# Two layers of a retention, HGRN2 and differential attention block: the 16-bit planes of the values are parted and joined on ScalarE instead of GpSimd

## Chip, cores and metric

The kernel runs on one core of a Trainium2 chip. The metric is the device time of one execution in microseconds (us). Of several executions the median is taken. A profiled execution gives the trace; its engines are called TensorE (PE), VectorE (DVE), ScalarE (ACT), GpSimd (POOL) and SyncE (SP, here only a queue that issues transfers).

## What is computed

A sequence of 16 learned tokens and 256 inputs (272 tokens, width 1024) goes through two layers. Each layer is a mixer and a convolutional feed-forward network, both with a residual and an RMS norm:

```python
proj = hn @ w_in                      # 12 parts: rq rk rv rg | hq hf hi hg | dq dk dv | mg
o_ret = retention(rq, rk, rv, rg)     # 4 heads, scores x fixed decay, values rv (256 wide)
o_hg  = hgrn2(hq, hf, hi, hg)         # 8 heads, decay from the data, values hi (128 wide)
o_da  = diff_attention(dq, dk, dv)    # 8 heads, two softmaxes, values dv (128 wide)
y = sum(sigmoid(mg)[n] * (o[n] @ w_branch[n]) for n in (ret, hg, da))
h = h + y @ w_out
...
u = rms_norm(h) @ w_ffn_in            # 2 x 2816 wide
c = causal convolution of width 3 over the tokens
h = h + (silu(gate) * val) @ w_ffn_out
```

All inputs and results are float32. The output is the normed last 256 tokens.

## The kernel before

**Layout.** Activations lie transposed in SBUF: the partitions hold 128 features, the free dimension the 272 tokens. A projection takes 128 x 128 weight tiles as the stationary operand and 272 tokens as the moving one. In the second layer most projections leave out the first 14 tokens (258 columns).

**Weights.** To keep float32 accuracy, every weight tile and every activation is split into a rounded high part and a remainder, and each product is made of three matmuls (lines 915 to 917: high with high, high with low, low with high). The weights come as one stream of chunks of 8 tiles (class `_Weights`, method `next`, line 626). For each chunk the SP queue loads `wraw` (3 buffers), ScalarE copies it to `whi` (4 buffers) and VectorE subtracts to get `wlo` (4 buffers). So for each chunk there is a chain: load, ScalarE, VectorE, TensorE. A load must wait until VectorE is done with the chunk three before, a split until TensorE is done with the chunk four before.

**Order of the projections.** `ORDER` (line 63) lists pairs of output tiles in the order in which TensorE makes them. Marks among them start (`+`) and end (`!`) the work of the heads that is spread between the projections: `hga` and `hgb` are the two groups of four HGRN2 heads, `hgoa` and `hgob` their outputs, `ret` the retention heads, `daa` and `dab` the attention heads.

**The values.** The heads need the values with tokens on the partitions, so the projections `rv`, `hi` and `dv`, 4 pairs of tiles each, must be transposed: 12 pairs in a layer, 24 in all. `values` (line 1389) evacuates a pair from PSUM to `vsrc` on ScalarE, and `to_tokens` (line 951) transposes its first 256 tokens. Each float32 is treated as two 16-bit halves. The lower and upper halves are parted into two planes (`apart`), each plane is transposed by a DMA issued from the SP queue (`turned`), and the two planes are joined again into float32 words in `vt` (or `rvt`). Parting and joining are plain copies with a step of two 16-bit words on one side, 512 elements in each partition; each is one instruction for each plane. The last 16 tokens of a pair go another way: GpSimd gathers them in `tails`, and TensorE transposes those.

**The level chain of HGRN2.** `hg_heads` (line 1064) computes the data-dependent decay by levels of 1, 2, 4, ... 64 tokens. At each level TensorE multiplies blocks of keys and queries (`lev`, line 1107), VectorE puts the masked result into `near`, and VectorE then multiplies the next level's decays into `hq` and `hf` in place. Before that, on the four lowest levels, ScalarE copies the last tokens of `hf` and `hq` to `kt` and `qt`, and once a larger part of `hq` to `extra`. At the end ScalarE copies the blocks to `at`. Retention and HGRN2 outputs take their norm over partitions by an all-reduce on GpSimd (`hr`), with ScalarE before and after it.

**The planner.** The kernel does not issue instructions as the program text runs. Class `_Plan` (line 357) collects them with their dependences, a due time (`key`) and a cost, plays the engines forward as a list scheduler (`order`, line 454), and issues everything in the order found. Each engine then works through its own list in that order, and waits where an operand isn't ready. The costs are fixed in the code:

```python
act = _Engine(plan, nc.scalar, "act", 0.094, 0.833e-3)
...
pool = _Engine(plan, nc.gpsimd, "pool", 0.04, 0.85e-3)
sync = _Engine(plan, nc.sync, "sp", 0.06, 4 / 360e3)
```

To these come, for GpSimd, 1.6e-3 us for each element in a partition (line 592), and for a transfer 2.0 us from the end of its issue to landing (line 546). For a copy of 512 elements the planner thus reckons 0.52 us on ScalarE and 1.29 us on GpSimd, for the transpose of a plane 0.79 us on the SP queue and 2.0 us more.

Of the kernel before, what the change touches and what calls it, by code (L numbers as in the profile page):

```python
# [16 lines left out]
AF = mybir.ActivationFunctionType  # L17
# [4 lines left out]
P = 128  # L22
# [644 lines left out]
def _trace(ctx, tc, plan, a, depth, probe):  # L667
    nc = tc.nc
    act = _Engine(plan, nc.scalar, "act", 0.094, 0.833e-3)
    dve = _Engine(plan, nc.vector, "dve", 0.068, 1.042e-3)  # L670
    pe = _Engine(plan, nc.tensor, "pe", 0.0, 4 / 2400)
    pool = _Engine(plan, nc.gpsimd, "pool", 0.04, 0.85e-3)
# [14 lines left out]
    def new(pool_, shape, dt, tag, bufs, name):  # L687
        serial[0] += 1
        return plan.tile(pool_, shape, dt, tag, bufs, f"{name}_{serial[0]}")
# [16 lines left out]
    def temp2(tag, bufs=2):  # L706
        return temp(2 * T, tag, bufs).rearrange("p (a t) -> p a t", a=2)
# [243 lines left out]
    def to_tokens(src, vt, e):  # L951

        def planes(name):
            return new(tp, [P, 4 * T], U16, "vsrc", 4, name)[:, : 8 * P].rearrange("p (i x) -> p i x", i=2)

        apart, turned = planes("apart"), planes("turned")
        halves = lambda t, i: t.bitcast(U16).rearrange("p a (x two) -> p a x two", two=2)[:, :, :, i]
        for i in range(2):
            pool.tensor_copy(apart[:, i].rearrange("p (c f x) -> p c f x", c=2, f=2),
                             halves(src[:, :, : 2 * P], i).rearrange("p f (c x) -> p c f x", c=2))  # L960
        for i in range(2):
            sync.dma_start(turned[:, i].rearrange("p (b x) -> p b x", x=P), apart[:, i], transpose=True)
        for i in range(2):
            pool.tensor_copy(halves(vt[:, :, e : e + 2 * P], i), turned[:, i].rearrange("p (c x) -> p c x", c=2))

    def tail_tokens(tails):

# [21 lines left out]
    for li in range(depth):  # L989
# [399 lines left out]
        def values(ps, vt, e):  # L1389

            src = temp2("vsrc", 4)
            evacuate(src, ps)
            plan.key += 2.0
            to_tokens(src, vt, e)
            return src
# [57 lines left out]
        for name, j in ORDER:  # L1453
# [31 lines left out]
            if name in BASE:  # L1485
# [23 lines left out]
                elif name == "rv":  # L1509
# [3 lines left out]
                    src = values(ps, st["rvt"][j // 2], (j % 2) * 2 * P)  # L1513
# [4 lines left out]
                elif name in ("hi", "dv"):  # L1518
# [7 lines left out]
                    src = values(ps, st[f"{n}t{b}"], (j % 2) * 2 * P)  # L1526
# [39 lines left out]
            elif name == "fi":  # L1566
# [10 lines left out]
                c = temp2("two_b")  # L1577
# [8 lines left out]
                c = c[:, :, first:]  # L1586
# [43 lines left out]
```

## Time and profile before

| | |
|---|---|
| median of 3 runs | 1304.77 us (1304.16 to 1307.01) |
| the profiled execution | 1305.7 us |
| its span, first to last instruction | 1303.9 us |
| mean granted TensorE clock | 0.998 of full speed |
| busy: PE, DVE, ACT, POOL | 99%, 76%, 60%, 21% of the span |
| chain that ended last: PE, DVE, ACT | 88%, 9%, 1% of the span |
| HBM read | 216.16 MB, 167 GB/s over the span |

How to read the rows below: a row of a group names the line, the engine, the operation, output and inputs with their shapes (partitions x elements), the count, then busy time, the mean of one in ns, and the idle time of the engine just ahead of them with what ended it. Most operations pass through one helper, so line 607 stands for many; the tile names tell them apart. A row of the waits names who waited for whom, the total in us, how often, and the longest. A row of the timeline has start and duration in us, and in brackets the idle time ahead of it. Matmuls are pipelined and their records overlap, so a busy TensorE is not one at its peak, and spans on GpSimd are rough.

### The profile page before, as it was taken

To read this page: it belongs to the slowest core of one execution; us is meant where nothing else is said; L and a number is where in the kernel's file an instruction comes from. 1 tells how busy PE (TensorE), PEld (TensorE's weight loads), DVE (VectorE), ACT (ScalarE), POOL (GpSimd) and SP (SyncE) were. 2 spreads that over 40 slices of the span, in tenths; PEclk is the share of its full clock that TensorE was granted. 3 is DMA by queue.
4 is the path that set the end of the run, shared out by engine and by line. 5 is a ranking of instruction groups with operands and counts; after the bars stand their busy time and mean duration, and the time that the engine had idled before them with its cause. 6 is when DMAs were issued, how large, how long until landed. Compare 5 with 4: busy or idle time off the path is not lost.

```text
span 1303.9 us, 28637 instructions
## 1 busy us (share of the span) xinstructions
PE 1285.8 (99%) x11678; PEld 1256.7 (96%) x11678; DVE 986.7 (76%) x1589; ACT 786.7 (60%) x1282; POOL 270.3 (21%) x300
## 2 busy tenths in 40 slices
PE   9999999999999999999999999999999999999998
PEld 9999989999999999999999999899999999999986
DVE  7685897798686789886575768877986867898843
ACT  6746444746576567666456474447466765776643
POOL 5021262423422020000030212634223220200000
PEclk9999999999999999999999999999999999999999
DMA  7664665643744545555555646655446446466653
GB/s 272 200 179 147 173 178 155 164 160 125 199 138 157 182 156 178 183 173 183 175 178 185 186 149 185 179 155 168 159 138 199 145 162 198 144 207 196 201 190 112
DMA packets 86868, 225.36 MB, mean 173 GB/s; under 512 B 32976, under 2 KB 33104, under 8 KB 86736
## 3 DMA queue, kind: packets, MB, share of 16 engines
q1 hardware_dynamic: 86448, 223.00, 55.3%
q8 instruction: 92, 1.51, 0.5%
q10 hardware_dynamic: 288, 0.52, 0.1%
q14 instruction: 40, 0.33, 0.1%
HBM read 216.16 MB, written 1.05 MB: 167 GB/s over the span
## 4 chain that ended last, share of the span: by engine, by line
PE 88%; DVE 9%; issue 1%; ACT 1%; DMA 0%; SPq 0%; DVEq 0%; ACTq 0%
PE main L915 26%; PE main L917 26%; PE main L916 25%; DVE wlo L607 2%; PE fo L1430 2%; PE fo L1431 2%; PE fo L1429 2%; DVE two_b L607 1%; DVE two_a L607 1%; PE lev L1107 1%; PE ds L1291 1%; PE ho L607 1%; PE ro L607 1%; PE do L607 1%; DVE two_c L607 1%
## 5 line engine op out<-in xcount | busy, mean ns | idle before, releaser
L915 PE MATMUL main<-xh,whi 128*128 128x272 f32 (+1 forms) x2368 | 682.6, 288 | 0.8 <-ACT whi L607 0.8
L917 PE MATMUL main<-xh,wlo 128*128 128x272 f32 (+1 forms) x2368 | 673.9, 285 | 1.3 <-DVE wlo L607 0.7
L916 PE MATMUL main<-xl,whi 128*128 128x272 f32 (+1 forms) x2368 | 673.3, 284 | 1.5 <-DVE xl L607 1.5
L607 DVE TENSOR_TENSOR wlo<-wraw,whi 128x1024 fp32r<-128x1024 f32 (+1 forms) x411 | 512.0, 1250 | 187.8 <-ACT whi L607 186.6
L607 ACT ACTIVATE whi<-wraw 128x1024 fp32r<-128x1024 f32 (+1 forms) x411 | 427.5, 1042 | 250.9 <-PE main L916 166.3
L917 PEld LDWEIGHTS main<-xh,wlo 128*128 128x128 f32 x2368 | 446.5, 189 | 3.1 <-DVE wlo L607 2.3
L916 PEld LDWEIGHTS main<-xl,whi 128*128 128x128 f32 x2368 | 446.6, 189 | 2.2 <-DVE xl L607 1.9
L915 PEld LDWEIGHTS main<-xh,whi 128*128 128x128 f32 x2368 | 446.7, 189 | 2.0 <-ACT whi L607 1.0
L607 POOL TENSOR_TENSOR y<-h,rstd 128x272 f32<-128x272 f32 x32 | 34.6, 1112 | 318.1 <-ACT rstd L607 318.1
L607 POOL PARTITION_ALL_REDUCE hr<-hsq x36 | 65.8, 1837 | 88.9 <-ACT hsq L607 85.9
L607 DVE SCALAR_TENSOR_TENSOR two_b<-main,small,two_b 128x256 f32<-128x256 f32 (+2 forms) x144 | 65.3, 487 | 24.4 <-ACT two_b L607 22.7
L607 POOL COPY apart<-vsrc 128x512 uint16<-128x512 uint16 x48 | 40.7, 867 | 145.2 <-ACT vsrc L607 145.0
L607 ACT ACTIVATE two_b<-main,small 128x272 f32<-128x272 f32 (+1 forms) x72 | 37.3, 566 | 23.8 <-PE main L917 22.7
L915 PE MATMUL main<-ghi,whi 128*128 128x272 f32 x176 | 51.0, 290 | 0.0
L916 PE MATMUL main<-glo,whi 128*128 128x272 f32 x176 | 50.6, 287 | 0.0
L917 PE MATMUL main<-ghi,wlo 128*128 128x272 f32 x176 | 50.3, 286 | 0.0
L607 POOL COPY vt<-turned 128x512 uint16<-128x512 uint16 x32 | 37.0, 1160 | 29.2 <-DMA turned<-apart 29.0
L915 PE MATMUL main<-b0hi,whi 128*128 128x272 f32 (+1 forms) x128 | 37.9, 296 | 0.0
L915 PE MATMUL main<-b1hi,whi 128*128 128x272 f32 (+1 forms) x128 | 37.8, 296 | 0.0
L915 PE MATMUL main<-yhi,whi 128*128 128x272 f32 (+1 forms) x128 | 36.4, 284 | 0.0
L917 PE MATMUL main<-b0hi,wlo 128*128 128x272 f32 (+1 forms) x128 | 36.4, 284 | 0.0
L917 PE MATMUL main<-yhi,wlo 128*128 128x272 f32 (+1 forms) x128 | 36.3, 284 | 0.0
(235 smaller groups left out, 1970.1 us busy)
## 6 DMA issues: line engine op xcount, KB each, us to landing
wraw<-in_w SPq DMA_DIRECT2D x402, 512.0 KB, 3.4
h<-in_h SPq DMA_DIRECT2D x4, 272.0 KB, 5.1
dec<-in_dec SPq DMA_DIRECT2D x2, 544.0 KB, 4.9
wraw<-in_w SPq DMA_DIRECT2D x4, 256.0 KB, 4.2
const<-in_const SPq DMA_DIRECT2D x1, 937.0 KB, 5.6
turned<-apart SPq DMA_TRANSPOSE x48, 4.0
gain<-in_gl SPq DMA_DIRECT2D x1, 512.0 KB, 5.1
out<-y ACTq DMA_DIRECT2D x2, 256.0 KB, 2.8
```

What stands on the lines that cost most here:

```text
L607: self.plan.add(self.name, lambda: f(*args, **kw), cost, outs, ins, args[2] if method == "activation" else None)
L915: nc.tensor.matmul(o, wh, hi, start=first, stop=False)
L916: nc.tensor.matmul(o, wh, lo, start=False, stop=False)
L917: nc.tensor.matmul(o, wl, hi, start=False, stop=last)
L1107: nc.tensor.matmul(o, keys, x, start=True, stop=True)
L1291: nc.tensor.matmul(ss[m][:, at : at + nk], q[half, hd, q0 : q0 + P], k[half, hd, :nk], start=True, stop=True)
L1429: nc.tensor.matmul(o, gh, wh, start=False, stop=False)
L1430: nc.tensor.matmul(o, gl, wh, start=False, stop=False)
L1431: nc.tensor.matmul(o, gh, wl, start=False, stop=end)
```

## The change

In `to_tokens`, the two partings and the two joinings of each pair become ScalarE activations with the function Copy; nothing else of the text changes. Shapes, tiles, buffers and the transposes' queue stay as they are. The planner, which knows each engine's costs, lays out a new order for all engines.

```diff
         for i in range(2):
-            pool.tensor_copy(apart[:, i].rearrange("p (c f x) -> p c f x", c=2, f=2),
-                             halves(src[:, :, : 2 * P], i).rearrange("p f (c x) -> p c f x", c=2))
+            act.activation(apart[:, i].rearrange("p (c f x) -> p c f x", c=2, f=2),
+                           halves(src[:, :, : 2 * P], i).rearrange("p f (c x) -> p c f x", c=2), AF.Copy)
         for i in range(2):
             sync.dma_start(turned[:, i].rearrange("p (b x) -> p b x", x=P), apart[:, i], transpose=True)
         for i in range(2):
-            pool.tensor_copy(halves(vt[:, :, e : e + 2 * P], i), turned[:, i].rearrange("p (c x) -> p c x", c=2))
+            act.activation(halves(vt[:, :, e : e + 2 * P], i), turned[:, i].rearrange("p (c x) -> p c x", c=2), AF.Copy)
```

## The prediction

> **What bounds the kernel now.** I read the page first, then the busy time by stage, then what TensorE itself waited for, then the operations that the change touches and those around them. The first two lines of the page:
>
> ```profile
> span 1303.9 us, 28637 instructions
> ...
> PE 1285.8 (99%) x11678; PEld 1256.7 (96%) x11678; DVE 986.7 (76%) x1589; ACT 786.7 (60%) x1282; POOL 270.3 (21%) x300
> ```
>
> TensorE is busy but for 18.1 us. A change to another engine can therefore save little; it can only cost what it puts ahead of TensorE. The operations to be moved lie in a few stages, and the busy time by stage shows them:
>
> ```profile
> core 0: us, PE busy (x) PEld busy (x) DVE busy (x) ACT busy (x) POOL busy (x), PEclk, DMA share, GB/s
> ...
> 150.00:180.00 30.00, 28.56 (x344) 27.85 (x342) 26.73 (x38) 15.39 (x25) 19.28 (x21) 1.00 0.74 198
> 180.00:210.00 30.00, 29.27 (x491) 28.49 (x492) 27.38 (x46) 13.93 (x24) 11.91 (x14) 1.00 0.73 176
> ...
> 240.00:266.00 26.00, 25.19 (x202) 24.85 (x201) 20.61 (x27) 18.89 (x28) 16.12 (x17) 1.00 0.59 151
> ...
> 830.00:860.00 30.00, 28.28 (x476) 27.27 (x474) 25.79 (x43) 12.67 (x23) 16.30 (x18) 0.94 0.76 185
> ...
> 895.00:917.00 22.00, 22.00 (x180) 21.83 (x178) 16.63 (x19) 15.57 (x26) 16.09 (x17) 1.00 0.59 165
> ```
>
> From 150 to 210 us and again around 830 to 860 VectorE is about 90% full while ScalarE is half idle; from 240 to 266 and 895 to 917 ScalarE is itself about 72% full (18.89 of 26, 15.57 of 22), and these are the stages with the least room for more. TensorE's own waits between 60 and 1000 us, where all values are handled:
>
> ```profile
> PE lev L1107 <- DVE hf L607: 3.2, 2, 1.7
> PE ho L607 <- DVE ho L607: 1.4, 2, 0.8
> ...
> PE lev L1107 <- DVE tot L607: 0.4, 1, 0.4
> PE lev L1107 <- DVE hq L607: 0.4, 1, 0.4
> ```
>
> They are few, and most are the level products (lev), which wait for VectorE.
>
> **What is moved, and its price.** 48 partings and 48 joinings (two 16-bit planes, 12 pairs of value tiles, 2 layers) leave GpSimd for ScalarE's queue.
>
> ```profile
> L607 POOL COPY apart<-vsrc 128x512 uint16<-128x512 uint16 x48 | 40.7, 867 | 145.2 <-ACT vsrc L607 145.0
> ```
>
> ```profile
> L607 POOL COPY vt<-turned 128x512 uint16<-128x512 uint16 x32 | 37.0, 1160 | 29.2 <-DMA turned<-apart 29.0
> L607 POOL COPY rvt<-turned 128x512 uint16<-128x512 uint16 x16 | 15.7, 1011 | 27.7 <-DMA turned<-apart 27.7
> ```
>
> ```profile
> L607 ACT ACTIVATE whi<-wraw 128x1024 fp32r<-128x1024 f32 (+1 forms) x411 | 427.5, 1042 | 250.9 <-PE main L916 166.3
> ```
>
> ```profile
> L607 ACT ACTIVATE extra<-hq 128x512 f32<-128x512 f32 x8 | 5.4, 675 | 3.5 <-DVE hq L607 3.5
> ```
>
> GpSimd is freed of 40.7 + 37.0 + 15.7 = 93.4 us. The trace has no 16-bit copy on ScalarE; the nearest row is a strided copy between SBUF tiles of the same 512 elements, 0.675 us. At that price ScalarE gains 96 x 0.675 = 65 us and goes from 786.7 to about 852. From below, half of what a split of 1024 elements takes (1.042 us) would be 0.52 us and 50 us in all; from above, if ScalarE needed what GpSimd needed for a joining (1.16 us), 111 us. I take 65, since the form is the same.
>
> Is that time on TensorE's path? The splits of the weights (whi) are what TensorE needs from ScalarE all the time:
>
> ```profile
> 69.82 0.29 PE L915 MATMUL main<-xh,whi 128*128 128x272 f32 x1
> ```
>
> ```profile
> 70.19 0.28 PE L915 MATMUL main<-xh,whi 128*128 128x272 f32 x1
> ```
>
> ```profile
> ACT whi L607 <- PE main L916: 166.3, 134, 2.9
> ```
>
> One weight tile lasts 0.37 us, a chunk of 8 tiles 2.96 us. 134 times ScalarE waited for TensorE before a split, that is, for one of the four whi buffers: it then stands three chunks ahead, 8.9 us. So a copy of 0.675 us in front of a split is hidden by that lead. If the lead were used up, the overfull stages would show: 240 to 266 gets 8 copies (two pairs), 18.89 + 5.4 = 24.3 of 26 us, and 895 to 917 gets 15.57 + 5.4 = 21.0 of 22. Full, but not over. The copies as such I cost at nothing. What stays on GpSimd comes no later than before, and I cost that at nothing too.
>
> **What is relieved.** GpSimd's copies and VectorE slow each other. Two VectorE products of the same shape, one alone and one beside a joining:
>
> ```profile
> 87.17 0.71 DVE L607 TENSOR_TENSOR hf<-hf,tot 128x544 f32<-128x544 f32 x1
> ```
>
> ```profile
> 89.69 1.24 DVE L607 TENSOR_TENSOR hf<-hf,tot 128x544 f32<-128x544 f32 x1
> ```
>
> ```profile
> 88.99 1.41 POOL L607 COPY vt<-turned 128x512 uint16<-128x512 uint16 x1 [2.26 <-DMA turned<-apart]
> ```
>
> The second costs 0.53 us more. If each of 96 copies did that once, VectorE would win 51 us; not every copy meets such an operation, so I take half, 25 us. What of it reaches the end is bounded by TensorE's waits for lev: 3.2 + 0.4 + 0.4 = 4.0 us, and by what followed the longest of them. In the stage from 830 to 860 the granted clock is 0.94 instead of 1.00, which over 30 us is 1.8 us. Together 5.8 us at most. But the same chain of levels runs through ScalarE: it copies kt and qt before VectorE may overwrite hf and hq. I take half, **-2.9 us**, and keep 0 and -5.8 as ends.
>
> **What is added: a wait in ScalarE's queue.** The joining waits for a DMA transpose. Behind GpSimd's joining stood little. Behind ScalarE's stand the splits whi, the evacuations of PSUM and the copies qt, kt, extra and at of the level chain, and for these wait VectorE and then TensorE, in order. The transposes and GpSimd's waits for them:
>
> ```profile
> turned<-apart SPq DMA_TRANSPOSE x48, 4.0
> ```
>
> ```profile
> POOL vt L607 <- DMA turned<-apart: 29.0, 21, 3.7
> POOL rvt L607 <- DMA turned<-apart: 27.7, 9, 6.4
> ```
>
> The order of all instructions comes from the kernel's own planner, which reckons a transpose at 0.06 + 0.73 us on the SP queue and 2.0 us more to landing, 2.8 in all. Measured it is 4.0 from issue to landing. And the issue itself comes late, since the SP queue is in order too. One episode:
>
> ```profile
> 831.17 1.66 POOL L607 COPY apart<-vsrc 128x512 uint16<-128x512 uint16 x2
> ```
>
> ```profile
> 838.46 1.93 POOL L607 COPY rvt<-turned 128x512 uint16<-128x512 uint16 x2 [4.41 <-DMA turned<-apart]
> ```
>
> ```profile
> 828.40 5.94 SPq L607 DMA_DIRECT2D wraw<-in_w  x3
> 834.45 3.44 SPq L607 DMA_TRANSPOSE turned<-apart  x2
> ```
>
> ```profile
> 835.19 0.21 ACT L607 ACTIVATE qt<-hq 128x32 f32<-128x32 f32 x1
> 835.49 0.26 ACT L607 ACTIVATE kt<-hf 128x64 f32<-128x64 f32 x1
> ```
>
> ```profile
> 832.50 0.73 PE L1107 MATMUL lev<-hq,hf 128*32 128x16 f32 x64 [1.70 <-DVE hf L607]
> 837.52 0.65 PE L1107 MATMUL lev<-hq,hf 128*32 128x16 f32 x56
> ```
>
> The planes are apart at 832.8, but the transposes stand behind a weight load and are issued at 834.45; they have landed at 838.46. A joining put where the planner thinks them landed (2.8 us after the parting, near 835.6) would hold ScalarE to 838.4, just where qt and kt of a level stand, for which the product at 837.52 waits.
>
> How much of such waits is hidden? The 21 waits at vt are 29.0 / 21 = 1.4 us each; I take them as hidden. The 9 at rvt are 3.1 us each, and they lie in the level stages. Hidden of each is at least the idle time that ScalarE has left per pair: from 150 to 180 it has four pairs, 16 copies, 30 - 15.39 - 10.8 = 3.8 us idle, 1 us per pair. At most it is the 2.8 us that the planner fills with other work. I take 2.0, in the middle: 27.7 - 9 x 2.0 = 9.7 us are not hidden on ScalarE. Of these I let two thirds arrive at TensorE (the rest is held by VectorE's other work in line): **+6.5 us**. With 1 us hidden it is (27.7 - 9) x 2/3 = 12.5, with 2.8 it is 1.7.
>
> **The sum.** The profiled execution took 1305.7 us (span 1303.9 and 1.8 around it). 1305.7 - 2.9 + 6.5 = 1309.3. It lies 0.9 above the median of the runs, 1304.77, so on the scale of the runs the forecast is **1308.4 us**.
>
> **Rivals.** *Faster: VectorE's relief decides.* The joinings come to stand where ScalarE is idle anyway (14.6 of 30 us from 150 to 180), nothing waits behind them, and VectorE, fuller than ScalarE in those stages, is what TensorE waits for. Then lev's waits and the slow clock go: 1304.8 - 5.8 = 1299.0. For it: all waits for lev are for VectorE. Against: kt and qt lie in the same chain. It decides if the joinings hold ScalarE under about 1.5 us each. The Trainium skill's page SBUF — State Buffer (Who interferes with whom) speaks for this rival: a VectorE instruction with two SBUF inputs and a GpSimd one that reads SBUF exclude each other, and the later one stands still until the earlier is done. The trace agrees in kind, with the 1.24 against 0.71 us above. *No change:* relief and waits cancel, or both stay in the lead of 8.9 us: 1304.8, within the 0.2% (2.6 us) that a measurement of this kernel can tell from none. *Much slower: ScalarE becomes the bound.* In the stages 240 to 266 and 895 to 917 only 1.7 and 1.0 us are left; two pairs in each, held at 3.1 us per pair, overrun by 4.5 and 5.2 us, and the four pairs from 150 to 180 by 12.4 - 3.8 = 8.6 us. If the lead is gone by then and half of these 18.3 us arrives on top of the forecast, it is 1317.6. Against: the lead is refilled between the stages. *That the change does not do what it says* I do not expect: the function is a plain copy, the one that whi uses beside every other function.
>
> **How the numbers follow.** Forecast (slower by some us) 0.40; much slower 0.10; no change 0.22; faster 0.28. So slower by over 0.2% has 0.50, within 0.2% 0.22, faster 0.28. The range goes from full relief with the least wait, 1304.8 - 5.8 + 1.7 = 1300.7, to 1317.6 and a little beyond for a dearer copy: 1300 to 1320. It leaves out about one in ten at each end. The slower cases alone span 1307.4 to 1320.
>
> **What would show it.** Right: GpSimd busy near 177 us, ScalarE near 852 with 96 copies of some 0.6 to 0.7 us; VectorE down by some 25 us; ScalarE waits named vt or rvt for the transposes of at least 30 us in total; TensorE's waits for lev or ho behind ScalarE or behind a VectorE operation that itself waited for qt, kt, extra or at. Wrong: waits for the transposes that are short on ScalarE, TensorE's waits for lev gone, and a granted clock of 1.00 throughout. A copy well over 0.7 us, or TensorE waiting for whi in the full stages, would mean the last rival.

## The result and the profile after

The changed kernel takes 1300.3 us in the median (1298.69 to 1302.91) against 1305.72 us of the kernel before beside it: a ratio of 0.9967, 95% interval 0.9957 to 0.9978. It is faster by a third of a per cent. The forecast was slower; its rival "VectorE's relief decides" gave 1299.0. The time lies at the lower end of the forecast's range, 1300 to 1320, and on the other side of the kernel before.

The page of the changed kernel, at the lines shown of before:

```profile
span 1296.9 us, 28609 instructions
...
PE 1284.4 (99%) x11678; PEld 1255.9 (97%) x11678; DVE 960.9 (74%) x1589; ACT 838.6 (65%) x1376; POOL 166.8 (13%) x204
```

The span is 7.0 us shorter than that of the profiled execution before, and TensorE's busy time 1.4 us: it waits less. VectorE, whose instructions are the same 1589, is busy for 25.8 us less. The stages, with the columns of the view in the prediction:

```profile
150.00:180.00 30.00, 30.00 (x415) 29.37 (x413) 25.12 (x41) 23.47 (x42) 5.27 (x7) 1.00 0.77 189
180.00:210.00 30.00, 29.84 (x437) 28.94 (x436) 23.29 (x43) 19.62 (x32) 0.42 (x2) 1.00 0.67 185
240.00:266.00 26.00, 26.00 (x214) 25.98 (x213) 19.05 (x30) 22.16 (x36) 9.14 (x10) 1.00 0.63 174
...
830.00:860.00 30.00, 30.00 (x559) 28.81 (x559) 26.02 (x52) 19.54 (x35) 0.53 (x3) 1.00 0.71 196
895.00:917.00 22.00, 22.00 (x184) 22.00 (x183) 18.87 (x30) 17.99 (x32) 9.19 (x7) 1.00 0.62 173
```

In the level stages TensorE now has hardly a gap, and the clock of the stage from 830 to 860 is 1.00, not 0.94. Comparing when TensorE begins the same weight tile in both traces, the changed kernel gains 2.1 us between 161 and 191 us, 1.2 by 276 us, loses 1 us by 335, and gains most of the rest between 805 and 880 us: the level stages of the two layers. TensorE's waits between 60 and 1000 us are now these, and none is for VectorE's part of the levels:

```profile
PE wt L607 <- DVE wts L607: 1.5, 2, 1.1
PE wt L1317 <- DVE two_a L607: 0.9, 2, 0.5
...
PE lev L1107 <- issue: 0.2, 1, 0.2
```

The moved copies, and ScalarE's waits for the transposes:

```profile
L607 ACT ACTIVATE apart<-vsrc 128x512 uint16<-128x512 uint16 x48 | 27.7, 620 | 0.8
L607 ACT ACTIVATE vt<-turned 128x512 uint16<-128x512 uint16 x32 | 24.9, 792 | 1.6 <-DMA turned<-apart 1.5
...
L607 ACT ACTIVATE rvt<-turned 128x512 uint16<-128x512 uint16 x16 | 11.9, 785 | 3.4 <-DMA turned<-apart 3.3
```

4.8 us of waits in all, where GpSimd had waited 56.7.

### The profile page after: what moved, and what is told of

Read it like the earlier page. It is cut to its first block, busy times and chain, and to the rows that moved or that the text cites. A ratio compares the mean times of both kernels' runs of the same rounds, so it can differ in the third digit from the quotient of the medians.

```text
span 1296.9 us, 28609 instructions
## 1 busy us (share of the span) xinstructions
PE 1284.4 (99%) x11678; PEld 1255.9 (97%) x11678; DVE 960.9 (74%) x1589; ACT 838.6 (65%) x1376; POOL 166.8 (13%) x204
## 4 chain that ended last, share of the span: by engine, by line
PE 91%; DVE 6%; issue 1%; ACT 1%; DMA 0%; SPq 0%; DVEq 0%
PE main L915 27%; PE main L917 26%; PE main L916 26%; PE fo L1430 2%; PE fo L1431 2%; PE fo L1429 2%; DVE wlo L607 1%; PE lev L1107 1%; DVE two_b L607 1%; DVE two_a L607 1%; PE ds L1291 1%; PE ro L607 1%; PE ho L607 1%; PE do L607 1%; DVE two_c L607 1%
## 5 line engine op out<-in xcount | busy, mean ns | idle before, releaser
L607 DVE TENSOR_TENSOR wlo<-wraw,whi 128x1024 fp32r<-128x1024 f32 (+1 forms) x411 | 502.7, 1229 | 192.2 <-ACT whi L607 185.5
L607 POOL COPY tails<-vsrc 128x32 f32<-128x32 f32 x32 | 10.6, 344 | 224.4 <-ACT vsrc L607 223.0
L916 PE MATMUL main<-b0lo,whi 128*128 128x272 f32 (+1 forms) x128 | 36.4, 284 | 0.0
L916 PE MATMUL main<-b1lo,whi 128*128 128x272 f32 (+1 forms) x128 | 36.3, 284 | 0.0
```

The costliest lines, as they stand in the source:

```text
L607: self.plan.add(self.name, lambda: f(*args, **kw), cost, outs, ins, args[2] if method == "activation" else None)
L916: nc.tensor.matmul(o, wh, lo, start=False, stop=False)
```

## Experiments

Two things changed at once: the engine that runs the copies, and the order of everything, since the planner laid it out anew. Theory A: GpSimd's copies slow VectorE, and taking them away is the gain. Theory B: the new order is the gain. Theory C: GpSimd's queue was in the way of its own all-reduces. Theory D is the step of the prediction: a joining that waits in ScalarE's queue holds up what stands behind it. The edits below are shortened. Each ratio is to executions of the kernel before in the same session.

**The new order, run by GpSimd.** The planner counts the copies as ScalarE's, GpSimd runs them.

```diff
+    on_pool = lambda out, x: nc.gpsimd.tensor_copy(out, x)
+    as_act = ("act", 0.094 + 0.833e-3 * 512)
...
+    plan.add(planned, lambda: run(out, x), cost, [out], [x])   # planned, cost = as_act; run = on_pool
```

> The planner counts the 96 copies as ScalarE's, at ScalarE's price, so every engine has the order of the changed kernel; but GpSimd runs them. Theory A (GpSimd's copies slow VectorE, and taking them away is the gain): VectorE busy back near 985 us, the waits for lev back, time 1304 to 1307. Theory B (the new order is the gain): time 1299 to 1302 with VectorE busy near 985. Theory C (GpSimd's queue was in the way of its own all-reduces): as A in time, but VectorE busy near 961.

Measured: 1311.13 us, ratio 1.0052 (1.0038 to 1.0066). The page's busy line and two of TensorE's waits (the line of lev is 1115 here):

```profile
PE 1285.4 (98%) x11678; PEld 1256.0 (96%) x11678; DVE 985.7 (75%) x1589; ACT 784.6 (60%) x1280; POOL 263.3 (20%) x300
```

```profile
PE lev L1115 <- DVE hf L607: 4.7, 3, 1.8
PE lev L1115 <- DVE tot L607: 2.0, 1, 2.0
```

VectorE's time and the waits for lev are back. The new order by itself is no gain but a loss, more than A had expected (1304 to 1307): B falls.

**The old order, run by ScalarE.** The mirror image: `as_pool` as the planner's engine and price, `nc.scalar.activation(out, x, AF.Copy)` as what runs.

> The mirror image: the planner counts the copies as GpSimd's, so the order is the one of before, and ScalarE runs them. Theory A: VectorE busy near 961 us, time 1299 to 1302 unless ScalarE's waits for the transposes cost something. Theory B: 1304 to 1307. Theory D (the step of the prediction: a joining at an unplanned place in ScalarE's queue holds up what stands behind it): ScalarE waits over 20 us for the transposes, time 1303 to 1312, slower than the changed kernel.

Measured: 1297.95 us, ratio 0.9951 (0.9939 to 0.9963).

```profile
PE 1283.9 (99%) x11678; PEld 1255.4 (97%) x11678; DVE 960.0 (74%) x1589; ACT 839.8 (65%) x1378; POOL 169.5 (13%) x204
```

```profile
ACT vt L680 <- DMA turned<-apart: 4.9, 5, 1.8
ACT rvt L680 <- DMA turned<-apart: 2.8, 5, 1.6
```

A again, a little faster than it had expected, and nothing of D: at places planned for another engine's queue the joinings waited 7.7 us, not over 20. With the kernel before and the changed one this makes a table of ratios:

| | GpSimd runs the copies | ScalarE runs them |
|---|---|---|
| old order | 1 | 0.9951 |
| new order | 1.0052 | 0.9967 |

The engine is worth 0.5% in the old order and 0.85% in the new one. The new order, which was laid out for ScalarE, costs 0.5% when GpSimd runs the copies; with ScalarE 0.16%, where the intervals overlap.

**The changed kernel, with GpSimd copying beside it.** GpSimd makes each copy too, into a tile that nothing reads.

```diff
+        def both():
+            run()
+            nc.gpsimd.tensor_copy(spare, x)   # spare in the shape of x
```

> The changed kernel, and for every one of the 96 ScalarE copies GpSimd makes the same copy from the same source into a spare tile that nothing reads. Order of all other engines as in the changed kernel. Theory A: VectorE busy 980 to 987 us, the gain gone, 1303 to 1306. Theory B: 1299 to 1302. Theory C: 1303 to 1306 too, with VectorE near 961.

Measured: 1311.14 us, ratio 1.005 (1.0034 to 1.0065).

```profile
PE 1289.6 (98%) x11678; PEld 1260.7 (96%) x11678; DVE 979.4 (75%) x1589; ACT 839.6 (64%) x1376; POOL 248.2 (19%) x300
```

```profile
POOL spare L682 <- DMA turned<-apart: 62.6, 29, 7.9
ACT rvt L607 <- DMA turned<-apart: 3.6, 4, 2.6
ACT vt L607 <- DMA turned<-apart: 2.2, 4, 0.8
```

The gain is gone, and more than the gain; it is as slow as the new order on GpSimd. The time lies above what A expected (1303 to 1306). VectorE is busy for 18.5 us more than in the changed kernel, just under what A expected. The three waits deserve a look: in one execution, for the same transposes, GpSimd waited 62.6 us and ScalarE 5.8.

**The same with fills in place of the copies.** GpSimd reads one element of the source and then fills 272 floats twice.

```diff
-            nc.gpsimd.tensor_copy(spare, x)
+            nc.gpsimd.tensor_copy(spare[:, :1], x[..., :1])
+            for _ in range(2):
+                nc.gpsimd.memset(spare.bitcast(F32)[:, 2:], 0.0)
```

> As the kernel with the copies beside, but in place of each copy GpSimd reads one element of the source and then fills a spare tile twice (272 floats each, about 0.65 us), so it is as busy but hardly reads SBUF. Theory A in its narrow form (it is the reading that excludes VectorE's second operand): VectorE busy 960 to 968 us, time 1299 to 1302. Theory A in its wide form (any work on GpSimd slows VectorE): VectorE near 985, 1303 to 1306. Theory B: 1299 to 1302. Theory C (GpSimd's queue): 1303 to 1306.

Measured: 1300.82 us, ratio 0.9979 (0.9966 to 0.9992).

```profile
PE 1283.9 (99%) x11678; PEld 1254.7 (97%) x11678; DVE 962.7 (74%) x1589; ACT 839.3 (65%) x1376; POOL 256.8 (20%) x492
```

Its group of fills, among GpSimd's groups by line:

```profile
L684 POOL MEMSET spare<- 128x272 f32 x192 | 62.7, 327 | 5.5
```

GpSimd is as busy as with the copies (256.8 against 248.2 us), waits for and holds the same tiles, and VectorE stands at 962.7, the time, within the intervals, at that of the changed kernel. So it is not GpSimd's work, nor its queue (C falls), but its reading of SBUF over the whole plane. Added up by operation, the copies beside lengthen VectorE's operations on two tensors (TENSOR_TENSOR) by 15.6 us over the changed kernel, the fills by none. This is the rule of the Trainium skill's page SBUF — State Buffer (Who interferes with whom): VectorE with two SBUF inputs contends with a GpSimd instruction that reads SBUF, not with one that only writes it. The two runs agree with it.

**One half of the change at a time.** Only the partings, or only the joinings, on ScalarE; the planner orders anew for each.

> Only the 48 partings are ScalarE's; the joinings stay on GpSimd, and the planner orders anew. Theory A (GpSimd's reading beside VectorE's two-operand work is the cost): GpSimd loses about 40 us of its 93, so VectorE busy falls by 40% of the full change's 25 us, to 973 to 979, and the time lies between the two kernels, 1300 to 1304, if the new order is as good as the old one. If the new order decides, any time from 1299 to 1309.

> Only the 48 joinings are ScalarE's. Theory A: VectorE busy falls by 60% of 25 us, to 968 to 974, time 1299 to 1303. ScalarE's waits for the transposes as in the full change, under 10 us. If a new order decides: 1299 to 1309.

Measured: partings 1302.81 us, ratio 0.9976 (0.9966 to 0.9986), VectorE busy 973.7 us; joinings 1304.0 us, ratio 0.9986 (0.9977 to 0.9995), VectorE 966.5 us, a little under what was expected. The partings came out as expected; the joinings are a little slower than the 1299 to 1303 expected, and ScalarE's waits for the transposes are 10.8 us there, not under 10. Each half gives a part of the gain, but not clearly in proportion to VectorE's relief: the joinings relieve VectorE more and by the best estimates gain less, though the intervals overlap. An order of its own goes with each half, and the table above shows that an order can be worth up to half a per cent, so the split between the halves is not settled by these two.

**Truer prices for the planner.** A transpose 1.2 + 2.5 us, a joining 0.69.

```diff
-            done = t + cost + (2.0 if e == "sp" else 0.0)
+            done = t + cost + (2.5 if op.func == "turn" else 2.0 if e == "sp" else 0.0)
...
+            plan.ops[-1].func, plan.ops[-1].cost = "turn", 1.2   # behind the transpose's dma_start
...
+            plan.ops[-1].cost = 0.69                             # behind the joining
```

> The changed kernel with prices nearer to the trace in the planner: a transpose 1.2 us on the SP queue and 2.5 us to landing (before 0.79 and 2.0), a joining 0.69 us (before 0.52). If the changed kernel lost its 2.4 us against the old order because joinings are planned too early, this gives 1297 to 1299.5 and ScalarE's waits for the transposes go under 3 us. If the difference of orders is an accident of the list scheduler, anything from 1297 to 1303.

Measured: 1298.37 us, ratio 0.9947 (0.9934 to 0.9961); ScalarE's waits for the transposes 3.4 us. The time is the one that the first expectation named, but the waits went from 4.8 only to 3.4 us, not under 3, and an accident of the scheduler would allow that time too. It is level with the old order on ScalarE; both are ahead of the kernel before by some half a per cent, and their best estimates ahead of the changed kernel.

**A later landing.** One more transpose of the first plane, into a spare tile, ahead of the real ones of each pair.

```diff
+                    nc.sync.dma_start(spare.rearrange("p (b x) -> p b x", x=P), apart[:, 0], transpose=True)
                     run()    # the first real transpose of the pair
```

> The changed kernel in its own order, but ahead of the first transpose of each pair the SP queue issues one more, of the same plane into a spare tile, so that both planes land about 1.25 us later and the loads behind them as well. Theory D (a joining that waits in ScalarE's queue holds up TensorE, two thirds of the wait arriving): ScalarE waits 20 to 35 us for the transposes, time 1306 to 1320. Theory A with ScalarE's lead of some 9 us: the waits grow as much, but the time only to 1300 to 1304.

Measured: 1311.21 us, ratio 1.0041 (1.0028 to 1.0054). ScalarE's waits, and those of TensorE that grew (lev is line 1116):

```profile
ACT rvt L607 <- DMA turned<-apart: 18.1, 11, 3.6
ACT vt L607 <- DMA turned<-apart: 16.2, 14, 2.8
```

```profile
PE lev L1116 <- issue: 2.3, 1, 2.3
PE lev L1116 <- DVE hf L607: 2.0, 3, 0.8
PE lev L1116 <- ACT extra L607: 1.9, 1, 1.9
```

Now that ScalarE waits 34.3 us, the kernel is slower by 0.7% than the changed one. TensorE waits for `extra`, one of the copies that the prediction had put behind a joining. Behind a joining that had waited, two partings and two splits were in line before it:

```profile
835.31 0.80 ACT L607 ACTIVATE rvt<-turned 128x512 uint16<-128x512 uint16 x1 [1.67 <-DMA turned<-apart]
835.97 1.13 ACT L607 ACTIVATE apart<-vsrc 128x512 uint16<-128x512 uint16 x2
837.00 1.99 ACT L607 ACTIVATE whi<-wraw 128x1024 fp32r<-128x1024 f32 x2
838.89 0.65 ACT L607 ACTIVATE extra<-hq 128x512 f32<-128x512 f32 x1
```

Time and waits are what D expected. But the extra transposes may cost something by themselves, so there is a control.

**The same transposes behind.** The extra transpose is issued after the second real one.

> The control for the kernel with late landing: the same 24 extra transposes, but issued behind the two real ones of each pair. The loads behind them are put off as much, the planes' landing hardly. If it was the joining's wait in ScalarE's queue that cost 11 us there: ScalarE waits 4 to 12 us for the transposes, time 1299 to 1303. If it was the fuller SP queue or the DMA engines: 1308 to 1313.

Measured: 1306.81 us, ratio 1.0004 (0.9995 to 1.0013): between the two expectations. ScalarE's waits are 8.6 us, as expected, yet the gain is gone. Where it went is seen on TensorE: the waits, then two rows of its timeline and the SP queue's row beside them.

```profile
PE lev L1116 <- issue: 5.8, 3, 2.2
```

```profile
839.14 0.43 PE L1116 MATMUL lev<-hq,hf 128*32 128x16 f32 x27
841.76 0.51 PE L1116 MATMUL lev<-hq,hf 128*32 128x16 f32 x37 [2.20 <-issue]
```

```profile
838.90 1.84 SPq L969 DMA_TRANSPOSE spare<-apart  x1
```

TensorE stops for 2.2 us after 27 of 64 small products of one block, though a block waits only at its start, and the rows show nothing that it waits for. The three stops of this kind at lev (181, 839 and 846 us) begin while a transpose is being issued, but this is not what they have in common with those of other runs. The trace's records of single transfers and instructions show what TensorE waits for: its own instructions. One queue of the page brings them in transfers of 16 KB, 92 of them for the 23515 instructions of PE and PEld, so some 256 at a time:

```profile
q8 instruction: 92, 1.51, 0.5%
```

Counted from the first, all three stops stand at the same place of a block of 256 instructions, and each ends 1.3 to 1.5 us after such a transfer has ended:

| stop, us | transfer ended, us | first instruction behind the stop, number in its block |
|---|---|---|
| 181.42 to 182.97 | 181.55 | 193 |
| 839.56 to 841.76 | 840.28 | 194 |
| 846.37 to 848.40 | 847.06 | 193 |

The same holds for every stop of TensorE over 0.25 us that is put down to "issue" in the profiles of all the kernels here, twelve in all: number 193 or 194, 1.25 to 1.5 us after a transfer. In the level stages with their many small products such transfers follow each other in as little as 3.8 us, elsewhere in some 15, so there a late one shows. Whether it is the extra transposes that make them late is not shown: the kernel with the joinings alone has no extra ones and has two such stops.

```profile
PE lev L1107 <- issue: 2.6, 2, 1.9
```

So of the loss with the late landing, 0.74% against the changed kernel, half (0.37%, 4.8 us) comes in the control with few of the waits, and the stops there, 5.8 us, are enough to account for it. The other half goes with 34.3 - 8.6 = 25.7 us more of waits, some 0.19 us for each us. That split is rough, as the stops fall differently in the two: 5.8 us in the control, 2.3 us with the late landing. With the stops taken out of both, the waits cost (4.8 + 5.8 - 2.3) / 25.7, some 0.3 us for each us.

**The small copies too.** With the truer prices, the 32 copies of the last tokens (`tails`) go to ScalarE as well.

> The kernel with the truer prices, and the 32 small copies of the last tokens (tails, 10 to 12 us of GpSimd's time) also made by ScalarE. By theory A VectorE's busy time falls by 1 to 4 us more; TensorE's waits for VectorE in these stages are nearly gone already, so the time stays at 1297 to 1300.

Measured: 1298.76 us, ratio 0.9947 (0.9934 to 0.9961), VectorE 958.6 us against 961.1. VectorE gains a little more, the time nothing: TensorE had hardly a wait for VectorE left there that this could shorten.

## Why the prediction was wrong

**What held.** The bound by TensorE; the copies' own time, hidden by ScalarE's lead (838.6 us against the 852 reckoned; its records overlap where one follows another); VectorE's relief, 25.8 us against 25, though that was half of 51 by choice, not by count, and so close by luck; the price of a parting, 0.62 us against 0.675; that full stages around 240 and 895 us would still do. GpSimd fell to 166.8 us, not 177: its copies of `tails`, which were not moved, take 10.6 us where they took 20.9. A joining cost 0.79 us. The Trainium skill's page ScalarE: Activation LUTs (What ACT_TABLE_LOAD costs) gives 186 ns and 0.833 ns for each element, by which a copy of 512 is estimated at 0.61 us: the partings agree, the joinings take nearly 30% more.

**The step that failed** is the term "what is added": +6.5 us from GpSimd's waits for the transposes, of which 9.7 us were to remain on ScalarE. ScalarE's waits are 4.8 us in all, before anything is hidden. A wait in the trace is the time between the engine's arrival and the landing. GpSimd had little else in its queue and arrived early; ScalarE has other work ahead of a joining and arrives late. The copies beside show it, 62.6 against 5.8 us for the same landings. Nor did the transposes simply land sooner: in the old order on ScalarE they take 3.8 us in the median, nearly the 4.0 of before, and ScalarE waits 7.7 us. And the order kept the level chain ahead of the joining. The prediction feared for qt and kt at one episode; this is that place in ScalarE's timeline now:

```profile
835.24 0.23 ACT L607 ACTIVATE qt<-hq 128x32 f32<-128x32 f32 x1 [0.57 <-DVE hq L607]
835.64 1.07 ACT L607 ACTIVATE whi<-wraw 128x1024 fp32r<-128x1024 f32 x1 [0.17 <-PE main L916]
836.61 0.24 ACT L607 ACTIVATE kt<-hf 128x64 f32<-128x64 f32 x1
838.91 1.43 ACT L607 ACTIVATE rvt<-turned 128x512 uint16<-128x512 uint16 x2 [2.06 <-DMA turned<-apart]
```

The joining did wait there, for 2.06 us, but behind qt and kt, and ahead only of work with a lead. The mechanism itself was not wrong: with 34.3 us of waits the kernel loses. Nor was its price far off: the prediction named waits of at least 30 us as the sign of its +6.5, at most 0.22 us for each, and the pair of runs with extra transposes gives 0.19 to 0.3, roughly. What failed is the size of the waits. Whether two thirds of what is not hidden arrive, these runs do not show.

**The relief was halved without need.** It was taken as -2.9 us with -5.8 as the end, since kt and qt lie in the same chain. In the profiled executions all of the waits of lev for VectorE went, the low clock too, and the span lost 7.0 us; but the one of the changed kernel is the fastest of its six. The medians differ by 5.4, near the full -5.8.

**The planner** was seen only as the source of early joinings. That a new order by itself can cost was nowhere in the sum: it costs half a per cent when GpSimd runs it; on ScalarE it hid a part of the gain, if anything.

**The right rival** was given 0.28. It was the one that the rule of the Trainium skill's page SBUF — State Buffer spoke for. The sign to follow was in the trace: VectorE was about 90% full, ScalarE half idle, and of TensorE's waits for the products of the levels 4.0 us were for VectorE. The prediction says that all were; there is one more, for ScalarE's `qt`, and it is short:

```profile
PE lev L1107 <- ACT qt L607: 0.3, 1, 0.3
```

## What to carry to other kernels

A wait is a property of the engine that arrives, not of the thing waited for: before moving a waiting instruction, ask what the new engine has ahead of it, not how long the old one stood. Copies on GpSimd that read SBUF are paid for by VectorE's two-operand work; where VectorE is nearly full and what TensorE waits for, a half-idle ScalarE is the better place. Where a planner lays out the order, run old order with new engine and new order with old engine, since an edit that changes both shows only their sum.

## What the runs showed of the hardware

Plane copies that read SBUF on GpSimd lengthen VectorE's work beside them by 18 to 26 us in all (979.4 and 986.7 against 960.9 us busy), while fills and one-element reads that keep GpSimd as busy do almost nothing (962.7). A copy of 512 16-bit words on ScalarE takes 0.62 us when its output is dense and 0.79 us when its output has a step of two words. TensorE can stop for some 2 us in the middle of a block of 64 small products, with no wait that the views name: its instructions come 256 at a time in transfers of 16 KB, and it goes on 1.25 to 1.5 us after the transfer has ended (twelve stops over 0.25 us, all at the same place of a block of 256 instructions).
